# A two-layer decoder trunk on one core: the emptying of the values' bank written one step later, and the first quarter of the output products split by halves

## The chip, the cores and the metric

The kernel runs on one core of one Trainium2 chip. The metric is the device time of one execution in microseconds (us), the median over runs. TensorE (PE in the profile) does the matmuls, VectorE (DVE), ScalarE (ACT) and GpSimd (POOL) the elementwise work, and SyncE (SP) issues most transfers.

## The reference

The kernel computes two layers over 1024 tokens of width 1024, in float32. Each layer projects its input to a main part, memory queries and two gates, computes the main part and an attention over 256 memory tokens, multiplies both with their gates, projects back (the output products) and normalises. In the first layer the main part is a causal pooling. In the second it is an attention with 16 heads of 64 and a forget gate, and that is where the first half of the change lies:

```python
def block(args):                      # 128 queries at a time, all 16 heads
    logits = jnp.einsum('bqhd,bkhd->bhqk', qi, k) * scale
    logits = logits + (ci[..., :, None] - cum_k[:, :, None, :])
    logits = jnp.where(mask[None, None], logits, -jnp.inf)      # causal
    p = jax.nn.softmax(logits, axis=-1)
    return jnp.einsum('bhqk,bkhd->bqhd', p, v)
...
y = jnp.concatenate([y_main * silu(g_main), y_mem * silu(g_mem)], axis=-1)
x = layer_norm(ALPHA * x + y @ w_out, ln_g, ln_b)
```

## The kernel before

To keep float32's precision, each operand is split into a high part and a remainder, and each product is a sum of two or three cheaper matmuls. In the output products the parts are called `hi` (fp32r), `lo` (the remainder, bfloat16) and `top` (a bfloat16 copy); the three terms are hi x hi ("high"), and top x lo and lo x top ("low_top").

**The attention** is the function `fox`. It runs over 16 heads, and in each head over 8 steps, one for each tile of 128 queries, from tile 7 down to tile 0. Tile i has (i + 1) x 128 keys, cut into one or two parts of at most 512 columns (`parts_at`). A step does the following:

- `mask` (L1009, GpSimd) prepares the masked forget rows of a tile three steps ahead.
- `probs` computes the logits on TensorE (L323, two matmuls for each part, into one of three banks "L"), then on VectorE the scaled and masked logits with their running minimum (L1035), which frees the bank, and then on ScalarE the exponentials (L1043) into one of two banks "T". Between the two it normalises the tile of the step before (`inverse`, and `halves`: a scaled copy on ScalarE, L1071, and its remainder on VectorE, L1072).
- `fill.pump` places matmuls of projections (L359) between, so that TensorE always has work; their weights are split on GpSimd (L176, L193, L178).
- `turn` issues the transposing transfer of the probabilities (SyncE, L1088).
- Six steps after its tile, `values` multiplies the transposed probabilities with the values (L1097). It does so for four tiles at a time, so in two steps of each head, and accumulates in the bank "O", of which there is one. Behind the matmuls it empties the bank with what is called the join here: ScalarE scales one half of the partitions into `o` (L1114), and VectorE adds the other half (L1115).
- After the second head of a pair, `pair_out` multiplies `o` with its gate on GpSimd (L1124) and, after the second four tiles, stores it to `y1d` (SyncE, L1126).

After the last head six more steps finish the values, and the output products of the memory part's first quarter (`lead`) serve as filling.

**The output products** (`OutProj.rest`) run over four quarters `sp` of two 128-row tiles each and over three chunks `c` of the mixed channels. For each pair (sp, c) they load 4 x 128 x 256 values to `src`, split them with `hi_lo` (ScalarE L198 for `hi`, VectorE L199 for `lo`, ScalarE L200 for `top`), and issue 48 matmuls (L599). The quarter's first chunk 2 is done early, by `lead`, so `rest` begins with (0, 0). For chunk 0 the low and top terms come first, for the others the high terms.

**What sets the order.** TensorE's order in the second layer is the written one (`manual_schedule(engines={PE})`). The queues of the other engines are put together at compile time by a planner, which issues, of the instructions that it takes to be ready, the one that was written first. `tc.keep_in_program_order` (also called `pin`) holds an instruction behind the one written before it on the same engine. The join is not pinned; the masks and the gating are.

Of the kernel before, what the change touches and what calls it, by code (L numbers as in the profile page):

```python
# [9 lines left out]
F32 = mybir.dt.float32  # L10
# [4 lines left out]
AF = mybir.ActivationFunctionType  # L15
ALU = mybir.AluOpType
AX = mybir.AxisListType

P = 128
# [3 lines left out]
ST = S // P  # L23
NH = 512
HEADS = 16
# [47 lines left out]
def run(units):  # L73
    for _ in units:
        pass
# [3 lines left out]
def trunk_kernel(ctx, tc, x, xT, memT, win, wk, wv0, wv, wmk, wmv, wout, poolw, pscale, lng, lnb, bforget, out):  # L79
# [5 lines left out]
    nc = tc.nc  # L85
# [109 lines left out]
    def hi_lo(to, src, pinned=False, top=None):  # L195

        pin = tc.keep_in_program_order if pinned else lambda ins: ins
        pin(nc.scalar.copy(to.hi, src))  # L198
        pin(nc.vector.tensor_tensor(to.lo, src, to.hi.bitcast(F32), ALU.subtract))  # L199
        pin((top or nc.scalar.copy)(to.top, src))  # L200
# [343 lines left out]
    class OutProj:  # L544
# [36 lines left out]
            accs = [ps([P, NH], *bank) for bank in banks]  # L581
            return accs[:2], accs[2:]

        def products(self, accs, c, ys, apart=False):

            high, low_top = (0,), (1, 2)
            if apart:
                order = [(a, nh, part) for a in range(2) for part in (high, low_top) for nh in range(2)]
            else:
                order = [  # L590
                    (a, nh, part) for part in ((low_top, high) if c == 0 else (high, low_top))
                    for a in range(2) for nh in range(2)
                ]
            for a, nh, part in order:
                for i in part:
                    for k in range(4):
                        kt = 4 * c + k
                        y, w = three(ys[:, k, a * P : (a + 1) * P], self.ws[nh][kt // 2][kt % 2])[i]
                        nc.tensor.matmul(  # L599
                            accs[a][nh], y, w, start=kt == 8 and i == 0, stop=kt == 7 and i == 2,  # L600
                        )
                        yield NH
# [12 lines left out]
        def rest(self, resid, X, dst):  # L615
            order = [(sp, c) for sp in range(ST // 2) for c in (2, 0, 1)]
            accs, splits, gb = {}, [24], []
            if self.accs:
                accs[0], order[:6], splits = self.accs, [(0, 0), (1, 2), (0, 1), (1, 0), (1, 1)], [16, 24]
            if X is not None:  # L620
                self.split(splits.pop())

            def loads():

                for v in (lng, lnb):
                    t = sb([P, D], "P", 4)
                    nc.sync.dma_start(t, v[self.l].partition_broadcast(P))
                    gb.append(t)

            for sp, c in order:  # L630
                if c == 2:
                    accs[sp] = self.open((("T", 2), ("T", 2), ("L", 3), ("O", 1))) if 0 in accs and sp == 1 else self.open()
                src, ys = T([P, 4, 2 * P], F32), parts_of(T, [P, 4, 2 * P])
                nc.sync.dma_start(src, self.yd[c, :, :, sp * 2 * P : (sp + 1) * 2 * P])
                hi_lo(ys, src)
                if splits:
                    self.split(splits.pop(0), X is None)
                if not gb and not splits:
                    loads()
                if c == 1:  # L640
                    zs = rows_of(resid, sp)
                run(self.products(accs[sp], c, ys, X is None and sp == ST // 2 - 1 and c == 1))
                if X is not None and (sp, c) == (0, 0):
                    scale_of_norm(gb)
                if X is not None and c == 0 and sp:
                    scales_of_weights(sp - 1)
                if X is not None and c == 0 and sp in (1, 2):
                    keep(sp - 1)
                if c == 1:
                    norm(sp, accs.pop(sp), gb, zs, X, dst)  # L650
# [40 lines left out]
    X = parts_of(stream, [P, KT, S])  # L691
# [110 lines left out]
    X = X1  # L802
    with tc.tile_pool(name="in1", bufs=1) as in1:
# [165 lines left out]
        gs = {}  # L969
# [49 lines left out]
        def probs(hd, i, R, sums, inverse, behind):  # L1019

            q, kx, ky = pairs[hd // 2][hd % 2]
            qs = slice(i * P, (i + 1) * P)
            p = MK([P, S], F32)
            C, parts = diagonal.pop((hd, i)), parts_at(i)
            m = tiny(2)
            top = -NEG  # L1030
            for n, (lo, up) in enumerate(parts):
                lg = ps([P, NH], "L", 3)[:, : up - lo]
                mm3(lg, ((q[:, qs], kx[:, lo:up]), (q[:, qs], ky[:, lo:up])))
                rows = C[:, : up - lo] if n == len(parts) - 1 else R[:, lo:up]
                nc.vector.tensor_tensor_reduce(p[:, lo:up], lg, rows, unq, top, ALU.add, ALU.min, m[:, n : n + 1])  # L1035
                top = m[:, n : n + 1]
                if n == 0:
                    inverse()
            behind()
            es = []  # L1040
            for n, (lo, up) in enumerate(parts):
                e = ps([P, NH], "T", 2)[:, : up - lo]
                nc.scalar.activation(  # L1043
                    e, p[:, lo:up], AF.Exp, bias=top, scale=-1.0, accum_out=sums[:, n, hd % 2, i : i + 1],
                )
                es.append((lo, up, e))
            return hd, i, es, sums
# [42 lines left out]
        def values(hd, c, o):  # L1090

            v, un, b = pairs[hd // 2][2], unv if hd >= 4 else unv0, hd % 2
            acc = ps([P, NH], "O", 1)
            blocks = [(i, j) for i in range(4 * c, 4 * c + 4) for j in range(i + 1)]

            def add(rows, i, j, e, first, last):
                nc.tensor.matmul(  # L1097
                    acc[rows, (i % 4) * P : (i % 4) * P + P], v[:, b, 2 * j : 2 * j + (1 if e else 2), :].rearrange("p e d -> p (e d)"),
                    pt[hd, i][:, e * (i + 1) + j, :], start=first, stop=last,
                )  # L1100

            def highs(opens):
                for i, j in blocks:
                    add(slice(0, P), i, j, 0, opens and (i, j) == blocks[0], not opens and (i, j) == blocks[-1])

            def lows(opens):
                for k, (i, j) in enumerate(blocks):
                    add(slice(64 * (k % 2), 64 * (k % 2) + 64), i, j, 1, opens and k < 2, not opens and k >= len(blocks) - 2)

            for n, part in enumerate((lows, highs) if c else (highs, lows)):  # L1110
                part(n == 0)
            own, other = slice(64 * b, 64 * b + 64), slice(64 - 64 * b, P - 64 * b)
            oc = o[own, c * NH : (c + 1) * NH]
            nc.scalar.activation(oc, acc[other, :], AF.Copy, scale=un[own])  # L1114
            nc.vector.scalar_tensor_tensor(oc, acc[own, :], un[own], oc, ALU.mult, ALU.add)  # L1115

        bfb = const.tile([P, HEADS], F32, name="bfb")
        nc.sync.dma_start(bfb, bforget.partition_broadcast(P))
# [1 line left out]
        def pair_out(pr, c, o, g):  # L1120

            for k in (2 * c + 1, 2 * c) if g is not None else ():
                cols = slice(k * 2 * P, (k + 1) * 2 * P)
                tc.keep_in_program_order(nc.gpsimd.tensor_tensor(o[:, cols], o[:, cols], g[:, cols], ALU.mult))  # L1124
            if c == 0:
                nc.sync.dma_start(y1d[pr // 4, :, pr % 4, :], o)  # L1126
# [13 lines left out]
        def fox(following, out_proj, head):  # L1140
            fill, past, fresh = Fill(), [None] * LAG, [None]

            def two_lines(row):
                return [lines[0][:, row + j, :].bitcast(F32) for j in range(2)]

            ahead_R = forget_rows(0)
            for i in range(3):
                mask(0, ST - 1 - i, ahead_R)
            for hd in range(HEADS + 1):
# [16 lines left out]
                for i in range(ST if hd < HEADS else LAG):  # L1166
# [12 lines left out]
                    def behind():  # L1179
                        if fresh[0]:  # L1180
                            split.append(halves(*fresh[0]))
                            fresh[0] = None
# [21 lines left out]
                    if hd < HEADS:  # L1204
                        new = (hd, tile_of, o)
                        fresh[0] = probs(hd, tile_of, R, sums, inverse, behind)
                    else:
                        inverse()
                        behind()
                        out_proj.split(11 + i, True, gp_copy)  # L1210
                        if i > 1:
                            out_proj.fetch_two(two_lines(4 + 2 * i))
# [6 lines left out]
                        turn(*what)  # L1219
                    older = past[0]  # L1220
                    if older and older[1] % 4 == 0:
                        values(older[0], older[1] // 4, older[2])
                        if older[0] % 2:
                            pair_out(older[0] // 2, older[1] // 4, older[2], gs.get(older[0] // 2))
                    fill.pump(part * (1 - FRAC[0]))
                    past = past[1:] + [new]
                if b or hd == HEADS:
# [76 lines left out]
```

## Time and profile before

| | |
|---|---|
| time of three runs | 1190.94 us median (1190.53 to 1192.67) |
| profiled execution, its own time | 1189.29 us |
| its span | 1187.6 us |
| TensorE / VectorE / ScalarE / GpSimd busy | 98% / 66% / 58% / 24% of the span |
| granted TensorE clock, mean | 0.995 |
| attention | from about 640 us to 1060 us |
| output products of the second layer | from 1061 us |

Rows of the profile give a start and a duration in us, the engine, the line of the kernel, the operation, and the tiles it writes and reads (output<-inputs) with the shape. A bracket at the end is the idle time of the engine ahead of the instruction and what ended it. "PEld" is TensorE's loading of weights, which overlaps its matmuls. A group such as "x4" shows the time from the first start to the last end.

### The profile page before, as it was taken

To read this page: it belongs to the slowest core of one execution; us is meant where nothing else is said; L and a number is where in the kernel's file an instruction comes from. 1 tells how busy PE (TensorE), PEld (TensorE's weight loads), DVE (VectorE), ACT (ScalarE), POOL (GpSimd) and SP (SyncE) were. 2 spreads that over 40 slices of the span, in tenths; PEclk is the share of its full clock that TensorE was granted. 3 is DMA by queue.
4 is the path that set the end of the run, shared out by engine and by line. 5 is a ranking of instruction groups with operands and counts; after the bars stand their busy time and mean duration, and the time that the engine had idled before them with its cause. 6 is when DMAs were issued, how large, how long until landed. Compare 5 with 4: busy or idle time off the path is not lost. (4 is left out here: it accounts for less than half of the span.)

```text
span 1187.6 us, 19845 instructions
## 1 busy us (share of the span) xinstructions
PE 1165.6 (98%) x6941; PEld 671.7 (57%) x6941; DVE 779.1 (66%) x1840; ACT 684.8 (58%) x1512; POOL 285.5 (24%) x437
## 2 busy tenths in 40 slices
PE   8999999999999999999999999999999999999996
PEld 5566776555555557556674555555555545455553
DVE  5744675555765567457655888778877787874654
ACT  6578875976563234467422776667766667764210
POOL 3321001310000000000012454555555444750000
PEclk9999999999999999999999999999999999999998
DMA  7576646754385554446734889989996899875530
GB/s 257 182 242 193 170 105 213 245 180 144 91 279 162 158 148 131 122 134 117 192 130 113 181 187 208 202 167 198 204 207 145 168 196 203 215 193 168 176 108 35
DMA packets 286196, 203.89 MB, mean 172 GB/s; under 512 B 224912, under 2 KB 238352, under 8 KB 286096
## 3 DMA queue, kind: packets, MB, share of 16 engines
q1 hardware_dynamic: 279696, 181.59, 60.9%
q0 software_dynamic: 6400, 21.04, 5.5%
q8 instruction: 54, 0.88, 0.3%
q14 instruction: 46, 0.38, 0.1%
HBM read 116.01 MB, written 22.61 MB: 117 GB/s over the span
## 5 line engine op out<-in xcount | busy, mean ns | idle before, releaser
L359 PE MATMUL pj<-A,w 128*128 128x512 f16 (+2 forms) x2896 | 663.0, 382 | 3.3 <-ACT w L198 0.8
L359 PEld LDWEIGHTS <-w 128*128 128x128 f16 (+1 forms) x2560 | 245.4, 98 | 279.9 <-issue 9.6
L1043 ACT ACTIVATE T<-MK,s 128x512 f32<-128x512 f32 x192 | 111.2, 579 | 64.6 <-DVE s L1035 47.6
L1072 DVE SCALAR_TENSOR_TENSOR P<-T,s,P 128x512 f16<-128x512 f32 x192 | 111.9, 612 | 39.1 <-ACT P L1071 38.0
L1071 ACT ACTIVATE P<-T,s 128x512 f16<-128x512 f32 x192 | 103.0, 575 | 53.3 <-issue 28.9
L599 PEld LDWEIGHTS <-T 128*128 128x128 bf16 x736 | 70.7, 98 | 88.8 <-issue 4.4
L1009 POOL TENSOR_SCALAR_AFFINE_SELECT raw<-R 128x256 f32<-128x256 f32 (+3 forms) x128 | 59.3, 465 | 178.6 <-DVE s L1035 97.7
L323 PE MATMUL L<-A 128*128 128x512 f16 (+3 forms) x384 | 84.4, 326 | 3.1 <-DVE s L1035 3.0
L199 DVE TENSOR_TENSOR w<-raw,w 128x512 bf16<-128x512 f32 x74 | 51.9, 702 | 54.2 <-ACT w L198 39.3
L892 POOL MEMSET G<- 128x128 f32 x1 | 0.2, 204 | 333.7 <-DVE V L541 333.7
L359 PEld LDWEIGHTS pj<-A,w 128*128 128x128 f32 x352 | 65.1, 188 | 17.4 <-ACT w L198 1.9
L199 DVE TENSOR_TENSOR T<-T,T 128x1024 bf16<-128x1024 f32 x23 | 28.1, 1220 | 71.0 <-PE pj L599 37.3
L178 POOL TENSOR_TENSOR w<-B,w 128x512 f16<-128x512 f32 x54 | 62.8, 1165 | 4.0
L323 PEld LDWEIGHTS <-A 128*128 128x128 f16 x384 | 37.3, 98 | 46.2 <-issue 4.8
L198 ACT CAST T<-T 128x1024 fp32r<-128x1024 f32 x23 | 24.1, 1047 | 64.0 <-DMA T<-y1d 35.4
L198 ACT CAST w<-raw 128x512 fp32r<-128x512 f32 x76 | 46.7, 615 | 24.4 <-DMA raw<-in_win_dram 10.8
L1097 PEld LDWEIGHTS <-V 128*64 128x64 f16 (+1 forms) x1152 | 50.6, 104 | 13.0 <-issue 5.6
L1097 PE MATMUL O<-T,V 128*64 128x128 f16 (+1 forms) x1152 | 57.5, 220 | 0.0
L599 PE MATMUL pj<-B,T 128*128 128x512 bf16 (+1 forms) x192 | 53.0, 385 | 0.0
L1035 DVE CUSTOM_DVE_ANT_0 MK<-L,R,scales 128x512 f32<-128x512 f32 x64 | 45.3, 708 | 9.8 <-PE L L323 9.4
L200 ACT CAST w<-raw 128x512 bf16<-128x512 f32 x78 | 48.2, 618 | 3.3 <-PE pj L359 1.9
L599 PE MATMUL L<-B,T 128*128 128x512 bf16 (+1 forms) x168 | 47.4, 394 | 1.1 <-ACT T L200 1.1
(289 smaller groups left out, 1844.3 us busy)
## 6 DMA issues: line engine op xcount, KB each, us to landing
raw<-in_win_dram SPq DMA_DIRECT2D x66, 256.0 KB, 3.4
W<-in_win_dram POOLq DMA_DIRECT2D x48, 256.0 KB, 4.1
R<-cumd SPq DMA_DIRECT2D x16, 512.0 KB, 4.5
B<-in_win_dram SPq DMA_DIRECT2D x15, 512.0 KB, 5.2
y0d<-Y SPq DMA_DIRECT2D x12, 512.0 KB, 4.3
raw<-in_wout_dram SPq DMA_DIRECT2D x24, 256.0 KB, 2.6
T<-y0d SPq DMA_DIRECT2D x12, 512.0 KB, 4.7
A<-A SPq DMA_DIRECT2D x24, 256.0 KB, 4.0
```

The source lines that it names most:

```text
L178: pin(nc.gpsimd.tensor_tensor(to.lo, src, to.hi, ALU.subtract))
L198: pin(nc.scalar.copy(to.hi, src))
L199: pin(nc.vector.tensor_tensor(to.lo, src, to.hi.bitcast(F32), ALU.subtract))
L200: pin((top or nc.scalar.copy)(to.top, src))
L323: nc.tensor.matmul(acc, a, b, start=i == 0, stop=i == len(terms) - 1)
L359: nc.tensor.matmul(accs[n], a[:, k, :], b[:, pc * 4 + k, n * NH : (n + 1) * NH], start=seen[n] == 1, stop=seen[n] == 3 * KT,)
L599: nc.tensor.matmul(accs[a][nh], y, w, start=kt == 8 and i == 0, stop=kt == 7 and i == 2,)
L1009: tc.keep_in_program_order(nc.gpsimd.affine_select(C[:, :w], R[:, lo:up], [[-1, w]], ALU.is_ge, -NEG, base=w - P, channel_multiplier=1,))
L1043: nc.scalar.activation(e, p[:, lo:up], AF.Exp, bias=top, scale=-1.0, accum_out=sums[:, n, hd % 2, i : i + 1],)
L1071: nc.scalar.activation(pair[:, lo:up], e, AF.Copy, scale=r)
L1072: nc.vector.scalar_tensor_tensor(pair[:, L + lo : L + up], e, r, pair[:, lo:up], ALU.mult, ALU.subtract)
L1097: nc.tensor.matmul(acc[rows, (i % 4) * P : (i % 4) * P + P], v[:, b, 2 * j : 2 * j + (1 if e else 2), :].rearrange("p e d -> p (e d)"), pt ...
```

## The change

The change has two parts. In the attention `values` no longer writes the join; it returns it as a function, and `fox` keeps it with its step in a list `unjoined`. The new function `joins` writes the join and, for the second head of a pair, `pair_out`. It is called behind the next step's `probs`. In the six steps after the last head it is called as soon as the values' matmuls are written.

In `rest` the pair (0, 0) of the second layer, whose chunk 2 was done early, splits its input by halves of 128 rows: two `hi` casts, each followed by its remainder, and then two `top` casts, all pinned. Its products take the high terms first.

```diff
-        def products(self, accs, c, ys, apart=False):
+        def products(self, accs, c, ys, apart=False, high_first=True):
...
-                    (a, nh, part) for part in ((low_top, high) if c == 0 else (high, low_top))
+                    (a, nh, part) for part in ((low_top, high) if not high_first else (high, low_top))
...
-                hi_lo(ys, src)
+                joins = bool(self.accs) and (sp, c) == (0, 0)
+                if joins:
+                    pin = tc.keep_in_program_order
+                    tiles = [(ys[:, :, a * P : (a + 1) * P], src[:, :, a * P : (a + 1) * P]) for a in range(2)]
+                    for to, y in tiles:
+                        pin(nc.scalar.copy(to.hi, y))
+                        pin(nc.vector.tensor_tensor(to.lo, y, to.hi.bitcast(F32), ALU.subtract))
+                    for to, y in tiles:
+                        pin(nc.scalar.copy(to.top, y))
+                else:
+                    hi_lo(ys, src)
...
-                run(self.products(accs[sp], c, ys, X is None and sp == ST // 2 - 1 and c == 1))
+                run(self.products(accs[sp], c, ys, X is None and sp == ST // 2 - 1 and c == 1, joins or c > 0))
...
-            nc.scalar.activation(oc, acc[other, :], AF.Copy, scale=un[own])
-            nc.vector.scalar_tensor_tensor(oc, acc[own, :], un[own], oc, ALU.mult, ALU.add)
+
+            def join():
+                nc.scalar.activation(oc, acc[other, :], AF.Copy, scale=un[own])
+                nc.vector.scalar_tensor_tensor(oc, acc[own, :], un[own], oc, ALU.mult, ALU.add)
+
+            return join
...
+            unjoined = []
+
+            def joins():
+                while unjoined:
+                    join, (h, k, o) = unjoined.pop()
+                    join()
+                    if h % 2:
+                        pair_out(h // 2, k // 4, o, gs.get(h // 2))
...
                         fresh[0] = probs(hd, tile_of, R, sums, inverse, behind)
+                        joins()
                     else:
                         inverse()
                         behind()
+                        joins()
...
-                        values(older[0], older[1] // 4, older[2])
-                        if older[0] % 2:
-                            pair_out(older[0] // 2, older[1] // 4, older[2], gs.get(older[0] // 2))
+                        unjoined.append((values(older[0], older[1] // 4, older[2]), older))
+                        if hd == HEADS:
+                            joins()
```

## Prediction

> **What bounds the kernel now.** I read the first part of the page, then TensorE's waits after the start of the forgetting attention (640 us) and after 1061 us, then the timeline around each wait. The page first:
>
> ```profile
> span 1187.6 us, 19845 instructions
> PE 1165.6 (98%) x6941; PEld 671.7 (57%) x6941; DVE 779.1 (66%) x1840; ACT 684.8 (58%) x1512; POOL 285.5 (24%) x437
> ```
>
> TensorE is busy for 98% of the span, so only 22 us of it are idle, and an edit that takes no matmul away can save only idle time of TensorE. Two rows of the view of waits (wait, total us, times, longest us) are where this change can reach:
>
> ```profile
> PE L L323 <- DVE s L1035: 3.0, 6, 1.1
> PE L L599 <- ACT T L200: 1.1, 1, 1.1
> ```
>
> The first row is from the attention. The logits' matmuls (L323) wait for one of the three banks "L", which the running minimum on VectorE (L1035) gives back. The second is the start of the output products. The timeline shows the first wait in one head (start, us, engine, line; idle time in brackets):
>
> ```profile
> 718.40 0.81 PE L323 MATMUL L<-A 128*128 128x512 f16 x4
> 719.44 1.41 DVE L1072 SCALAR_TENSOR_TENSOR P<-T,s,P 128x512 f16<-128x512 f32 x2 [0.80 <-ACT P L1071]
> 720.01 0.69 ACT L1114 ACTIVATE G<-O,scales 64x512 f32<-64x512 f32 x1
> 720.77 0.73 DVE L1115 SCALAR_TENSOR_TENSOR G<-O,scales,G 64x512 f32<-64x512 f32 x1
> 721.20 0.49 PE L323 MATMUL L<-A 128*128 128x384 f16 x2
> 721.42 0.73 DVE L1035 CUSTOM_DVE_ANT_0 MK<-L,R,scales 128x512 f32<-128x512 f32 x1
> 722.22 0.38 PE L323 MATMUL L<-A 128*128 128x256 f16 x2 [0.53 <-DVE s L1035]
> ```
>
> The four matmuls at 718.40 are the logits of tile 5. They have ended at 719.21. Their first minimum starts only at 721.42, because two remainders (L1072) and then the join's second half (L1115) stand before it in VectorE's queue. TensorE needs that bank for the second part of tile 4 and stands still until 722.22. So L1115 holds a bank that TensorE needs, and nobody needs its own result here. The same steps in another head:
>
> ```profile
> 742.84 1.41 DVE L1072 SCALAR_TENSOR_TENSOR P<-T,s,P 128x512 f16<-128x512 f32 x2 [0.80 <-ACT P L1071]
> 744.16 0.74 DVE L1035 CUSTOM_DVE_ANT_0 MK<-L,R,scales 128x512 f32<-128x512 f32 x1
> 745.17 0.76 DVE L1115 SCALAR_TENSOR_TENSOR G<-O,scales,G 64x512 f32<-64x512 f32 x1 [0.26 <-ACT G L1114]
> 746.96 0.71 PE L323 MATMUL L<-A 128*128 128x384 f16 x4
> ```
>
> Here the minimum stands directly behind the remainders and ahead of L1115, and the four matmuls of tile 4 run through without a wait. This head has longer steps, so it is not a clean trial, but it shows that VectorE's queue takes the minimum at this point as soon as L1115 is not chosen first.
>
> **Part one: the join behind the next step's exponentials.** It adds and removes no work in the attention. It writes the two join instructions (and, for odd heads, the gating on GpSimd and for the second half the store on SyncE) after the next step's minima, remainders and exponentials. Of 32 joins 30 move; the last two still follow their matmuls at once. TensorE's order is written by hand and stays. On VectorE and ScalarE an instruction that is written later gives way only where a rival is ready, so I take it that at 720.77 L1035 goes first and L1115 after it.
>
> What is that worth? The listed idle time is not all that is lost: the undisturbed four matmuls of tile 4 take 0.71, the disturbed ones 721.20 to 722.60, which is 1.40. The loss is 0.69, 0.16 more than the listed 0.53. The minimum can move ahead by at most the start-to-start of L1115 and L1035, 721.42 - 720.77 = 0.65. The other waits of this kind, each with the join before it:
>
> ```profile
> 697.24 0.76 DVE L1115 SCALAR_TENSOR_TENSOR G<-O,scales,G 64x512 f32<-64x512 f32 x1
> 698.84 0.38 PE L323 MATMUL L<-A 128*128 128x256 f16 x2 [0.27 <-DVE s L1035]
> 823.36 0.73 DVE L1115 SCALAR_TENSOR_TENSOR G<-O,scales,G 64x512 f32<-64x512 f32 x1
> 824.82 0.38 PE L323 MATMUL L<-A 128*128 128x256 f16 x2 [0.43 <-DVE s L1035]
> 925.96 0.73 DVE L1115 SCALAR_TENSOR_TENSOR G<-O,scales,G 64x512 f32<-64x512 f32 x1
> 927.41 0.38 PE L323 MATMUL L<-A 128*128 128x256 f16 x2 [0.44 <-DVE s L1035]
> 967.56 0.48 PE L323 MATMUL L<-A 128*128 128x384 f16 x2 [0.25 <-DVE s L1035]
> 973.46 0.73 DVE L1115 SCALAR_TENSOR_TENSOR G<-O,scales,G 64x512 f32<-64x512 f32 x1
> 974.91 0.38 PE L323 MATMUL L<-A 128*128 128x256 f16 x2 [1.12 <-DVE s L1035]
> ```
>
> The wait at 967.56 has no join before it; I leave it. The five others lose their idle time plus 0.16: 0.43, 0.69, 0.59, 0.60 and 1.28, together 3.59. Capped at 0.65 each, the change recovers 0.43 + 0.65 + 0.59 + 0.60 + 0.65 = 2.92 us. Of the last, 0.63 stays. What is late next is VectorE's second minimum of tile 5, and TensorE needs its bank only in the step behind, some 2.5 us later (718.40 to 721.20 is a step of 2.8), so the 0.73 us of L1115 fit there. Once regained, time stays regained, because TensorE waits for little else. I cost nothing for the bank "O", which is emptied later: the next values' matmuls in it are these:
>
> ```profile
> 728.59 1.12 PE L1097 MATMUL O<-T,V 128*128 128x128 f16 x20
> ```
>
> L1115 ended at 721.50, so 7.09 us are spare against a delay of about one step. If that cover were gone, each microsecond beyond it would be paid by TensorE. The Trainium skill speaks against this edit here ("PSUM — Partial Sum Buffer", section "Summary: rules for kernel authors": evacuate promptly, because PSUM is tight); I weigh it as the last rival.
>
> The cost that I cannot read off is on GpSimd, which has the masks, the weights' splits and the gating in one queue:
>
> ```profile
> 759.51 1.41 POOL L1124 TENSOR_TENSOR G<-G,G 128x256 f32<-128x256 f32 x2 [2.24 <-DVE G L1115]
> 763.09 2.27 POOL L178 TENSOR_TENSOR w<-B,w 128x512 f16<-128x512 f32 x2
> 764.33 3.19 PE L359 MATMUL pj<-A,w 128*128 128x512 f16 x14
> ```
>
> GpSimd waits 2.24 us for L1115 and then finishes a weight piece (half of the 2.27, so at about 764.23) only 0.1 before TensorE starts on it. The move puts the next step's mask ahead of the gating, which uses the idle time and helps. A later L1115 hurts if the splits stay behind the gating. The bounds are a gain of 0 (TensorE does not wait here now) and a loss of one step, 2.8. I take 0, because the 2.24 of idle time in front of the gating holds much of such a delay, and keep 2.8 for the range. SyncE's stores move with the gating; the transposes that share its queue are issued several steps ahead of the values that need them, so I cost them at nothing.
>
> **Part two: the first quarter of the output products.**
>
> ```profile
> 1058.48 0.39 PE L1097 MATMUL O<-T,V 128*64 128x128 f16 x8
> 1058.91 1.04 ACT L198 CAST T<-T 128x1024 fp32r<-128x1024 f32 x1 [5.34 <-DMA T<-y1d]
> 1059.25 0.59 PE L599 MATMUL pj<-B,B 128*128 128x512 bf16 x2
> 1059.86 1.04 ACT L200 CAST T<-T 128x1024 bf16<-128x1024 f32 x1
> 1059.98 1.23 DVE L199 TENSOR_TENSOR T<-T,T 128x1024 bf16<-128x1024 f32 x1 [3.68 <-ACT T L198]
> 1060.95 0.61 PE L599 MATMUL L<-B,T 128*128 128x512 bf16 x2 [1.11 <-ACT T L200]
> 1063.30 0.68 ACT L1114 ACTIVATE G<-O,scales 64x512 f32<-64x512 f32 x1
> 1064.01 0.62 ACT L198 CAST R<-A 128x512 fp32r<-128x512 f32 x1
> 1064.53 0.61 ACT L200 CAST R<-A 128x512 bf16<-128x512 f32 x1
> ```
>
> The pair at 1059.25 takes 0.59 with two matmuls of about 0.38, so their starts lie 0.21 apart and the next could start at 1059.67. It starts at 1060.95: 1.28 lost, since the low and top terms come first and need two whole casts (1058.91 to 1060.90). After the change the high terms come first and need half a cast. A cast of 512 takes 0.62, its next starts 0.52 later. But the casts are pinned behind what is written before them on ScalarE, and that is the last join, which now stands at 1063.30. It can run when the values end, 1058.87. So: L1114 1058.90 to 1059.58, the first half's cast 1059.50 to 1060.12, TensorE from about 1060.15. That recovers 0.80. The second half's cast (about 1060.64) is there before the first half's eight high matmuls end; low and top parts follow by 1062 and are needed after sixteen. Bounds: 1.28 if the join does not stand in front; 0 if the join waits for something else on the way. I take 0.80, the rows' own times. Cost: two casts become four, 4 x 0.52 against 2 x 0.95, or 0.2 us of ScalarE, hidden beneath 48 matmuls. The last join's result comes some 4 us earlier, which only helps the quarter that reads it:
>
> ```profile
> 1077.28 1.04 ACT L198 CAST T<-T 128x1024 fp32r<-128x1024 f32 x1 [4.85 <-DMA T<-y1d]
> 1082.03 0.81 PE L599 MATMUL L<-R,T 128*128 128x512 f32 x2
> ```
>
> Its cast is ready 3.7 us before TensorE asks, and after 1061 us the view of waits names no other wait of TensorE. So the 0.80 reaches the end.
>
> **Sum.** 2.92 + 0.80 = 3.72 us. The profiled execution took 1189.29 us (span 1187.6), so it would come to 1185.6. The three timed runs have a median of 1190.94, 1.65 above it; I carry the difference over: 1190.94 - 3.72 = 1187.2.
>
> **Rivals.**
> First, the join keeps its place. The queue is made at compile time; if the minimum is not held to be ready when L1115 is, the order stays as it is and only part two counts: 1190.94 - 0.80 = 1190.1. For it: the last join stands behind casts that were written later (1063.30), so the planner's idea of when things are ready differs from the chip's. Against it: at 744.16 it takes the minimum at this very point, and on the chip the logits have been there for 1.5 us.
>
> Second, GpSimd takes the wait over: the gating holds up the weights at 764.33 by a step, 2.8. That gives 1187.2 + 2.8 = 1190.0. For it: a spare of 0.1. Against it: one place only, and 2.24 of idle time before it.
>
> Third, slower: ScalarE's half of the join takes the wait's place.
>
> ```profile
> DVE P L1072 <- ACT P L1071: 38.0, 62, 0.8
> ```
>
> VectorE waits 62 times for ScalarE's scaled copies (L1071), and what stands behind it in the queue, minima included, waits too. If L1114 (0.69) lands in front of such a copy in the step behind, its minima move by about 0.65 there. That can be at each of the 15 first joins that move: 15 x 0.65 = 9.8, giving 1197.0. To outweigh 3.7 and the 2.4 of a measurable change it needs ten of them. For it: 38.0 us of such waits. Against it: most heads have no wait of TensorE at all, so they have slack for it.
>
> Fourth, the bank: the join sinks so far behind ready work that the next values' matmuls find "O" full. It decides from 7.1 us of delay, over two steps; at 8 us, were all 30 places as the one shown, 30 x 0.9 = 27, or 1214. That is what the page's rule would make of it. Against it: VectorE is busy for 66% of the span, so there is room within a step.
>
> **How the numbers follow.** About 0.2%, or 2.4 us, can be told from no change. Chances: forecast 0.58 (faster), order kept 0.17 and GpSimd 0.08 (both within 0.2%), ScalarE's half 0.13 and the bank 0.04 (slower). Faster 0.58, same 0.25, slower 0.17. The forecast's own range: 3.59 + 1.28 = 4.87 at best gives 1186.1, and 2.4 at least gives 1188.5. The range must take in the second and third cases (1190.1) and something for the spread of the runs (1190.53 to 1192.67): 1185.0 to 1191.5, which leaves the slower cases out.
>
> **What would show it.** Right: L1035 directly behind the second L1072 where L1115 now stands, the wait for L1035 down from 3.0 to about 0.8 (0.25 and some 0.5 of the longest one), and the first output product starting with high terms 0.8 earlier, behind L1114. Wrong: the same order with the same waits; TensorE waiting for L178 or L193 near 764; longer waits of L1072 for L1071 with new waits of TensorE behind them; or L1097 waiting for L1115.

## The result, and the profile after

The kernel with the change takes 1192.12 us (median of 22 runs, 1190.13 to 1193.9); the kernel before took 1190.76 in as many runs on the same chips. The ratio is 1.0014 [1.0007, 1.0020]: slower by 0.14%, where 1187.2 us and a gain were forecast. The profiled execution took 1192.17 us.

The page's first rows:

```profile
span 1190.5 us, 19846 instructions
PE 1166.6 (98%) x6941; PEld 672.2 (56%) x6941; DVE 779.0 (65%) x1841; ACT 684.9 (58%) x1514; POOL 284.5 (24%) x437
```

TensorE's waits after 640 us (wait, total us, times, longest us):

```profile
PE L L323 <- DVE s L1045: 6.2, 7, 1.5
PE pj L359 <- POOL w L193: 0.5, 1, 0.5
PE L L599 <- ACT T L640: 0.4, 1, 0.4
```

Line numbers have moved: the running minimum is L1045 (was L1035), the remainders L1082 (L1072), the join's halves L1126 and L1127 (L1114, L1115), the values' matmuls L1107 (L1097). Hardly any engine's busy time has changed (TensorE's by 1.0 us). The wait for the running minimum, which the change was expected to bring from 3.0 to about 0.8 us, is 6.2.

Two runs cannot be compared by their whole spans here: the time up to the attention's first logits matmul differs from run to run by more than the effect (644.3 to 647.6 us over all kernels below, by waits of TensorE near 8, 480 and 602 us that no edit touches). So I cut each trace at the start of the first logits matmul of every pair of heads. "Last" is the time from the last logits matmul to the first output product of `rest`; "whole" is from the start of the attention's first logits matmul to the start of the kernel's last matmul. Each trace is one execution, so the columns say what happened in that one, and the time says what the runs did together.

| us | pair 0 | pair 1 | pair 3 | pair 5 | pair 6 | pair 7 | last | whole |
|---|---|---|---|---|---|---|---|---|
| before | 42.58 | 47.05 | 46.41 | 46.42 | 47.50 | 54.39 | 18.50 | 531.93 |
| after | 42.35 | 47.02 | 46.43 | 46.43 | 48.05 | 56.42 | 17.83 | 533.73 |

Pairs 2 and 4 take 56.18 us in both. So part one won 0.26 us (pairs 0 and 1), part two 0.67, and 0.55 and 2.03 were lost in pairs 6 and 7, in which nothing had been expected to get longer; 0.11 more lies behind the first output product.

**Where the order stayed.** VectorE and TensorE in the head that the prediction took as its example, after:

```profile
719.95 1.41 DVE L1082 SCALAR_TENSOR_TENSOR P<-T,s,P 128x512 f16<-128x512 f32 x2 [0.81 <-ACT P L1081]
721.28 0.73 DVE L1127 SCALAR_TENSOR_TENSOR G<-O,scales,G 64x512 f32<-64x512 f32 x1
721.93 0.73 DVE L1045 CUSTOM_DVE_ANT_0 MK<-L,R,scales 128x512 f32<-128x512 f32 x1
722.73 0.38 PE L323 MATMUL L<-A 128*128 128x256 f16 x2 [1.04 <-DVE s L1045]
```

L1127 still stands ahead of L1045, although it is now written behind it. The same holds near 824, 926 and 974. Only near 676 and 698 did the two change places:

```profile
696.34 1.41 DVE L1082 SCALAR_TENSOR_TENSOR P<-T,s,P 128x512 f16<-128x512 f32 x2 [0.81 <-ACT P L1081]
697.67 0.74 DVE L1045 CUSTOM_DVE_ANT_0 MK<-L,R,scales 128x512 f32<-128x512 f32 x1
698.45 0.76 DVE L1127 SCALAR_TENSOR_TENSOR G<-O,scales,G 64x512 f32<-64x512 f32 x1
698.50 0.71 PE L323 MATMUL L<-A 128*128 128x384 f16 x4
```

There TensorE's four matmuls run through in 0.71 us, as forecast. But look at the next such place, 722.73: its listed wait grew from 0.53 to 1.04. TensorE came earlier by what it had won, VectorE did not, and most of the 0.43 won at 698 was given back one head later.

**Where new time is lost.** TensorE in head 13 (pair 6) and in head 15 (pair 7), after:

```profile
968.65 0.48 PE L323 MATMUL L<-A 128*128 128x384 f16 x2 [0.80 <-DVE s L1045]
1021.76 0.59 PE L323 MATMUL L<-A 128*128 128x512 f16 x2
1023.23 0.48 PE L323 MATMUL L<-A 128*128 128x384 f16 x2 [0.87 <-DVE s L1045]
1032.26 0.38 PE L323 MATMUL L<-A 128*128 128x256 f16 x2 [1.50 <-DVE s L1045]
```

The wait in head 13 is the one that the prediction left alone, listed with 0.25 before and 0.80 after: it is the whole 0.55 of pair 6. VectorE reaches it later. Its first minimum of head 12 starts 2.32 us behind the start of its logits (2.08 before), since one more remainder (L1082, 0.35 us) stands ahead of it. A few steps on it waits 1.10 us for a scaled copy (0.80 before), and from there it is 0.54 later than before.

The two waits in head 15 were not there before. With the 0.16 that a listed wait leaves out they cost 1.03 and 1.66. VectorE and GpSimd just ahead of them, with TensorE's matmuls beside them, first before, then after:

```profile
1016.75 1.66 POOL L193 TENSOR_SCALAR w<-B 128x512 f16<-128x512 f32 x2
1017.25 1.71 DVE L199 TENSOR_TENSOR MK<-A,MK 128x512 bf16<-128x512 f32 x2
1018.39 2.70 POOL L178 TENSOR_TENSOR w<-B,w 128x512 f16<-128x512 f32 x2
1020.03 1.47 PE L359 MATMUL pj<-A,w 128*128 128x512 f16 x6 [0.70 <-POOL w L178]
1020.40 0.80 DVE L1035 CUSTOM_DVE_ANT_0 MK<-L,raw,s 128x512 f32<-128x512 f32 x1
1021.33 0.92 PE L323 MATMUL L<-A 128*128 128x512 f16 x4
```

```profile
1015.45 0.76 DVE L1127 SCALAR_TENSOR_TENSOR G<-O,scales,G 64x512 f32<-64x512 f32 x1
1018.06 1.20 POOL L193 TENSOR_SCALAR w<-B 128x512 f16<-128x512 f32 x2
1019.23 2.72 POOL L178 TENSOR_TENSOR w<-B,w 128x512 f16<-128x512 f32 x2
1019.36 3.14 DVE L199 TENSOR_TENSOR MK<-A,MK 128x512 bf16<-128x512 f32 x2
1023.69 0.80 DVE L1045 CUSTOM_DVE_ANT_0 MK<-L,raw,s 128x512 f32<-128x512 f32 x1
```

L199 here is the remainder of two pieces of the output products' weights, an instruction that the change does not touch. Its two instructions (the L199 pair from here on) take 1.71 us before and 3.14 after. Before, the pair starts in front of GpSimd's last L193, and GpSimd is the one that takes longer (1.66 where after has 1.20). After, GpSimd's L178 starts 0.13 us ahead of it, and VectorE is the one. As a result the second minimum, which stood 0.93 us ahead of TensorE's logits (1020.40 against 1021.33), now stands 1.93 behind them (1023.69 against 1021.76). Half of that shift of 2.86, 1.43, is the longer L199. VectorE also starts L199 1.03 later against the first logits of head 15 (2.11 us behind them, 1.09 before), and the moved join of head 13 (L1127 at 1015.45; L1115 at 1012.40 before) now stands shortly ahead of it. Behind L199, 0.25 of this is caught up. And TensorE comes 0.65 earlier: its wait for L178 (0.70 listed at 1020.03, 0.86 in all) is gone, and a wait for L193 near 1018 is 0.22 longer. In TensorE's time this is 1.03 + 1.66 - 0.86 + 0.22 = 2.05, the loss of pair 7.

**The start of the output products**, after:

```profile
1060.87 1.12 PE L1107 MATMUL O<-T,V 128*128 128x128 f16 x20
1062.04 0.68 ACT L1126 ACTIVATE G<-O,scales 64x512 f32<-64x512 f32 x1 [5.35 <-PE O L1107]
1062.74 1.14 ACT L640 CAST T<-T 128x512 fp32r<-128x512 f32 x2
1063.41 0.73 PE L599 MATMUL L<-B,T 128*128 128x512 f32 x2 [0.45 <-ACT T L640]
```

The steps are those of the forecast: the join first, half a cast, then high terms. TensorE starts 1.42 us after the values' end (1061.99 to 1063.41), where 1.28 was worked out.

### The profile page after: what moved, and what is told of

It is laid out like the page before. It is cut to its first block, busy times and chain, and to the rows that moved or that the text cites. A ratio compares the mean times of both kernels' runs of the same rounds, so it can differ in the third digit from the quotient of the medians.

```text
span 1190.5 us, 19846 instructions
## 1 busy us (share of the span) xinstructions
PE 1166.6 (98%) x6941; PEld 672.2 (56%) x6941; DVE 779.0 (65%) x1841; ACT 684.9 (58%) x1514; POOL 284.5 (24%) x437
## 5 line engine op out<-in xcount | busy, mean ns | idle before, releaser
L1082 DVE SCALAR_TENSOR_TENSOR P<-T,s,P 128x512 f16<-128x512 f32 x192 | 111.6, 613 | 39.3 <-ACT P L1081 38.2
L1081 ACT ACTIVATE P<-T,s 128x512 f16<-128x512 f32 x192 | 102.7, 576 | 56.4 <-issue 34.7
L199 DVE TENSOR_TENSOR w<-raw,w 128x512 bf16<-128x512 f32 x74 | 51.9, 701 | 54.4 <-ACT w L198 39.2
L199 DVE TENSOR_TENSOR T<-T,T 128x1024 bf16<-128x1024 f32 x22 | 26.8, 1220 | 65.6 <-PE pj L599 43.8
L178 POOL TENSOR_TENSOR w<-B,w 128x512 f16<-128x512 f32 x54 | 62.9, 1166 | 3.7
L1107 PEld LDWEIGHTS <-V 128*64 128x64 f16 (+1 forms) x1152 | 50.6, 104 | 12.9 <-issue 5.7
L1107 PE MATMUL O<-T,V 128*64 128x128 f16 (+1 forms) x1152 | 57.5, 220 | 0.0
L1045 DVE CUSTOM_DVE_ANT_0 MK<-L,R,scales 128x512 f32<-128x512 f32 x64 | 45.3, 708 | 8.9 <-PE L L323 8.5
```

Source lines behind the costliest of these rows:

```text
L178: pin(nc.gpsimd.tensor_tensor(to.lo, src, to.hi, ALU.subtract))
L1081: nc.scalar.activation(pair[:, lo:up], e, AF.Copy, scale=r)
L1082: nc.vector.scalar_tensor_tensor(pair[:, L + lo : L + up], e, r, pair[:, lo:up], ALU.mult, ALU.subtract)
L1107: nc.tensor.matmul(acc[rows, (i % 4) * P : (i % 4) * P + P], v[:, b, 2 * j : 2 * j + (1 if e else 2), :].rearrange("p e d -> p (e d)"), pt ...
```

## The experiments

In the order in which they ran. "Whole" and "last" are the columns of the table above.

**Each part alone.** `b_only` writes every join at once, as before, and keeps part two; `a_only` keeps the joins of the change and takes part two away:

```diff
-                        if hd == HEADS:
-                            joins()
+                        joins()                     # b_only
...
-                joins = bool(self.accs) and (sp, c) == (0, 0)
+                joins = False                       # a_only
```

> Part two alone: every join is written at once behind its matmuls, as before; the first quarter of the output products is split by halves. Theory (the attention loses what part two gains): the attention's waits are those of the kernel before (3.0 us in 6 waits for L's minimum), the first output product waits about 0.5 instead of 1.1, and the time is 0.6 us below before (ratio 0.9995). Rival (part two itself disturbs the queues of the attention): waits for the minimum near 6 us as in the changed kernel, time 1 to 2 us above before.

> Part one alone: joins moved as in the change, the output products as before. Theory: about 2 us above before (the changed kernel's 1.4 and the 0.6 of part two), waits for the minimum near 6 us with the long ones behind 1020 us. Rival (the loss is part two's): the time of before within 0.5 us.

`b_only`: 1.0005 [0.9995, 1.0015] of before; whole 531.49, last 17.83, all pairs as before. `a_only`: 1.0015 [1.0006, 1.0024]; whole 533.23, pair 6 48.03, pair 7 56.49. So all of the loss is part one's. That part two alone is a gain rests on the trace (whole 0.44 us less than before); the time does not show the 0.6 us that were expected.

One number did not fit. In `a_only` the last stage is 17.39: 1.11 shorter than before without part two, and 0.44 shorter than after with it. The loads of the quarter show why. Before:

```profile
1053.43 1.51 SPq L634 DMA_DIRECT2D T<-y1d  x2
1057.75 1.12 PE L1097 MATMUL O<-T,V 128*128 128x128 f16 x20
```

with the cast at 1058.91, whose row stands in the prediction; and `a_only`:

```profile
1056.43 1.82 SPq L634 DMA_DIRECT2D T<-y1d  x2
1062.01 1.12 PE L1107 MATMUL O<-T,V 128*128 128x128 f16 x20
1062.05 1.04 ACT L198 CAST T<-T 128x1024 fp32r<-128x1024 f32 x1 [4.23 <-DMA T<-y1d]
```

The loads are issued 4.32 us ahead of the values' group of 20 before, and 5.58 ahead of it with part one, so the cast, which waits for the data, can start 1.12 us earlier. So with part one most of the wait that part two was made for is gone. SyncE's queue comes to these loads earlier: the transpose ahead of them takes 2.11 us before (at 1050.60) and 1.21 in `a_only` (at 1053.28). Which of the moved instructions brings this about was not isolated. Part two then put the join, which must wait for the values, in front of a cast whose data were there. Alone it wins 0.67; on top of part one it costs 0.44 in the traces, too little for the times to show (1.0014 and 1.0015).

**Which joins bring the loss of pair 7.** `ab_to11` moves only the joins of heads 0 to 11, `ab_from12` only those of 12 to 14:

```diff
-                        if hd == HEADS:
+                        if hd == HEADS or older[0] >= 12:     # ab_to11; ab_from12: < 12
```

> The change, but the joins of heads 12 to 15 are written at once as before. Theory (the loss comes late: the moved joins of the last two pairs shift VectorE's work so that two weight remainders of the output products run beside GpSimd's splits, and TensorE then waits about 2.7 us near 1023 and 1032 us): the two late waits go, the time is about 0.5 to 1 us below before. Rival (the loss is spread over the heads, by delayed joins in general): time still 1 us above before.

> The change with the joins of heads 0 to 11 written at once and only those of heads 12 to 14 moved. Theory (timing of VectorE against GpSimd at the end of head 14 decides, and any small shift of VectorE brings the collision): the last pair takes 55 to 56.5 us against 54.4 before. Rival (only moved joins of the earlier heads matter): 54.4.

`ab_to11`: 0.9993 [0.9983, 1.0003]; whole 533.61, pair 7 56.21. `ab_from12`: 1191.26 us in one run; whole 533.50, pair 7 56.43. In the traces each half alone brings nearly the whole loss, so the late joins as such are not its cause, and the two halves do not add up. The theory for `ab_to11` missed: both late waits of TensorE stayed (1.12 and 1.54 listed). What the halves have in common is the long L199 pair (`ab_to11`, then `ab_from12`):

```profile
1018.53 2.71 POOL L178 TENSOR_TENSOR w<-B,w 128x512 f16<-128x512 f32 x2
1018.53 3.27 DVE L199 TENSOR_TENSOR MK<-A,MK 128x512 bf16<-128x512 f32 x2
```

```profile
1018.28 2.72 POOL L178 TENSOR_TENSOR w<-B,w 128x512 f16<-128x512 f32 x2
1018.41 3.14 DVE L199 TENSOR_TENSOR MK<-A,MK 128x512 bf16<-128x512 f32 x2
```

In `b_only`, without the loss, L199 starts 1.14 us ahead of L178 and the pair takes 1.71, as before.

`ab_to11` isolates this best, because no join of pair 7 is moved in it. Up to 1.3 us ahead of the first logits of head 15, VectorE's rows lie where they lie before, within 0.01 us. What differs is GpSimd's start on a piece that a transfer brings (before, then `ab_to11`):

```profile
1015.00 1.78 POOL L176 TENSOR_SCALAR B<-B,scales 128x512 f32<-128x512 f32 x2 [4.01 <-DMA B<-in_win_dram]
```

```profile
1015.60 1.79 POOL L176 TENSOR_SCALAR B<-B,scales 128x512 f32<-128x512 f32 x2 [3.71 <-DMA B<-in_win_dram]
```

The logits start at 1016.16 and 1017.06, so L176 is 1.16 us ahead of them before and 1.46 here. It now starts ahead of another L199, which takes 1.07 for 0.69, and the L199 pair follows with 3.27 for 1.71. Together these two make VectorE's first minimum of head 15 lag 4.93 us behind its logits, 2.98 before. `b_only` and `b_split` issue this transfer at the same time against the logits, and there L176 starts 1.02 and 1.01 ahead. So the moment at which a transfer lands varies by more than what decides the order, and another execution of `ab_to11` may fall the other way. Its times do not show the loss that its trace has (0.9993; the trace has 1.68 more than before).

Pair 6 separates the halves: 48.05 in `ab_to11`, 47.52 in `ab_from12`. Its 0.55 does come from the joins up to head 11.

**The order forced.** `ab_pinned` takes VectorE's half of the join behind the step's first minimum and holds it there. ScalarE's half stays where it was before, and the second joins of each head are written at once:

```diff
+            nc.scalar.activation(oc, acc[other, :], AF.Copy, scale=un[own])
-            def join():
-                nc.scalar.activation(oc, acc[other, :], AF.Copy, scale=un[own])
-                nc.vector.scalar_tensor_tensor(oc, acc[own, :], un[own], oc, ALU.mult, ALU.add)
+            def join(pin=lambda ins: ins):
+                pin(nc.vector.scalar_tensor_tensor(oc, acc[own, :], un[own], oc, ALU.mult, ALU.add))
...
+                    first()        # in probs, behind a tile's first minimum: joins(tc.keep_in_program_order)
...
-                        if hd == HEADS:
+                        if hd == HEADS or older[1] // 4 == 0:
```

> ScalarE's half of each join stays directly behind the matmuls; VectorE's half of a head's first join is held in program order directly behind the next step's first minimum; the second join of each head stays where it was; part two kept. This forces the order that the forecast had taken for granted. The forecast's step: the waits for the minimum at about 698, 722, 825, 927 and 975 us shrink by 0.4 to 0.65 each, 2.9 in all, and with part two the time is 3.5 us below before. Rival (VectorE paces these heads, so TensorE only comes further ahead of it and waits later): single waits shrink, but others grow, and no more than 1.5 us of the 2.9 stays.

0.9984 [0.9974, 0.9994]; whole 530.31, the pairs 42.35, 46.41, 45.82 (pair 3), 45.82 (pair 5), 47.35 and 55.49. Near 824, in this kernel and then in the one after:

```profile
824.28 0.74 DVE L1045 CUSTOM_DVE_ANT_0 MK<-L,R,scales 128x512 f32<-128x512 f32 x1
824.78 0.71 PE L323 MATMUL L<-A 128*128 128x384 f16 x4
824.94 0.73 DVE L1129 SCALAR_TENSOR_TENSOR G<-O,scales,G 64x512 f32<-64x512 f32 x1
```

```profile
823.88 0.73 DVE L1127 SCALAR_TENSOR_TENSOR G<-O,scales,G 64x512 f32<-64x512 f32 x1
824.54 0.73 DVE L1045 CUSTOM_DVE_ANT_0 MK<-L,R,scales 128x512 f32<-128x512 f32 x1
825.33 0.38 PE L323 MATMUL L<-A 128*128 128x256 f16 x2 [0.45 <-DVE s L1045]
```

With the minimum first, the wait is gone. Pairs 0 to 6 win 2.21 us together, between the 2.9 of the theory and the 1.5 of the rival, so the mechanism of the prediction works where the order is the one that it took for granted. Two waits are left that it had counted as won or had left alone: 0.43 listed at 723.12 (0.53 before), and the one near 967, which cost 0.41 before and costs 0.80 here. Pair 7 of the heads still loses 1.10, beside an L199 pair of 3.26 us.

**The weights' splits moved.** To take L199 away from L178, `ab_split` writes the splits of these two pieces five steps later, with the joins of the change:

```diff
-                        out_proj.split((0, 0, 0, 0, 1, 3, 4, 6, 6, 6, 6, 6, 7, 8, 9, 10)[step], True, gp_copy)
+                        out_proj.split((0, 0, 0, 0, 1, 3, 4, 4, 4, 4, 4, 4, 6, 8, 9, 10)[step], True, gp_copy)
```

Here, and in `pinned_split` and `pinned_split_last` below, two pieces of the output weights are overwritten by the next ones before they are split, so the output products use other weights there; the number of recorded matmuls is the same (6894). `ab_split2` and the kernels after it also load the next ones one step later (13 for 12) and compute all of it.

> The change, with the two weight splits that fell in the last step of head 14 (rows 5 and 6 of the output weights) written five steps later, in a light step of head 15. Theory (these two remainders on VectorE run beside GpSimd's subtractions and take 1.6 us each instead of 0.7 to 1.1, so VectorE enters head 15 two microseconds late, and TensorE pays it at the next full bank): the last pair of heads takes about 54.4 us instead of 56.4, VectorE's lag at the start of head 15 falls from 5.0 to below 3.5, the time is about 0.5 us below before. Rival (the lag at head 15 comes from the moved joins of heads 13 and 14 themselves): the last pair still takes 56 us and the time stays 1.4 us above before.

> As ab_split, with the transfer that refills the rows of those two weights moved from step 12 to step 13, so that the split reads them first. Theory: last pair 53.8 us as in ab_split, and the time 0.2 to 0.3 us below before. Rival (ab_split was quick because of the weights that it missed): the last pair is back at 56 us.

`ab_split`: 1.0005 [0.9994, 1.0017], whole 531.67, pair 7 53.81. `ab_split2`: 0.9991 [0.9981, 1.0000], whole 531.37, pair 7 53.79. Pair 7 falls from 56.42 by 2.6 in both, so the weights that `ab_split` did not use are not why. The time of `ab_split` was not below before, as its theory had it; that of `ab_split2` is, at the edge of its interval. GpSimd and VectorE in `ab_split2`, at the place where L199 was:

```profile
1019.76 2.28 POOL L178 TENSOR_TENSOR w<-B,w 128x512 f16<-128x512 f32 x2
1020.05 0.74 DVE L1045 CUSTOM_DVE_ANT_0 MK<-L,R,scales 128x512 f32<-128x512 f32 x1
1021.32 0.80 DVE L1045 CUSTOM_DVE_ANT_0 MK<-L,raw,s 128x512 f32<-128x512 f32 x1
```

L178 takes 2.28 with nothing in its way. Against the first logits of head 15 (1017.72 here, 1017.25 after) the second minimum comes 2.83 us earlier than after. Is that a repair of the change's cost, or a gain of its own? `b_split` makes the same move without part one:

> Part two and the later split alone, every join at once as before. Theory (the later split only takes away the collision, which the kernel before mostly lacks): last pair 54.4 or up to 0.6 less, time 0.5 to 1 us below before. Rival (the later split is a gain of its own of 2 us whatever the joins do): last pair 52.5, time 2.5 us below before.

0.9975 [0.9964, 0.9985]; whole 530.52, pair 7 53.51. The kernel before had some of this cost too, 0.88 us in pair 7 (54.39 to 53.51): its wait for L178 is gone. That speaks for the theory, while the time comes out nearer to the rival's 2.5 us; the trace has 1.41 of it. With part one, pair 7 is 53.79: of the 2.03 that it lost, 0.28 is left, and this is TensorE's wait for L193 near 1018 (0.52 listed in `ab_split2`, 0.24 in `b_split`). So 1.75 hung on L199 in that place. The move takes away the pair's own work there too, so how much of the 1.75 is the 1.43 of standing still is not separated by these runs; in `ab_to11`, where VectorE came as before, the longer L199s alone went with 1.82 in pair 7.

**All of it together.** `pinned_split` joins the forced order and the later splits:

> VectorE's half of each head's first join held behind the next step's first minimum, ScalarE's half and the second joins as before, the two weight splits five steps later, part two kept. Theory: the first twelve heads keep their gain of 2.1 us, the last pair goes from 55.5 to about 54.4; with part two the time is about 3 us below before (ratio 0.9975). Rival (VectorE's work only moves, and head 15 pays for the splits where it is fullest): the last pair stays at 55.5 and the time is 1.5 us below before.

0.9975 [0.9964, 0.9986]; whole 529.16, pair 7 54.39. That is 1.10 less than `ab_pinned` in pair 7, as much as `ab_pinned` had lost there, but still 0.88 above `b_split`. The two waits for the minimum in head 15 (1.12 and 0.50 listed in `ab_pinned`) are gone; in this trace TensorE waits 1.06 for L193 near 1017 instead, where `b_split` has 0.24. `pinned_split_last` was to take the last join from in front of the half casts:

```diff
                     for to, y in tiles:
                         pin(nc.scalar.copy(to.hi, y))
                         pin(nc.vector.tensor_tensor(to.lo, y, to.hi.bitcast(F32), ALU.subtract))
+                    last_join()
                     for to, y in tiles:
                         pin(nc.scalar.copy(to.top, y))
```

> As pinned_split, and the very last join is written behind the first quarter's high casts, ahead of the top casts. Theory: the first output product no longer waits 0.4 for the cast, 0.6 us less than pinned_split. Rival (the later join holds up the store that the third product group reads): another wait of TensorE takes its place near 1080 us and nothing is gained.

0.9981 [0.9969, 0.9993]; last stayed 17.84. The edit had moved VectorE's half only; ScalarE's, which stands in front of the cast, was still where it had been. So this run tells nothing of the wait. `pinned_split_last2` moves both halves of that one join:

> As pinned_split_last, with both halves of the very last join behind the high casts (the run before had moved only VectorE's half, and ScalarE's still stood in front), and the refill as in ab_split2. Theory: the wait of the first output product goes, 0.6 us less than pinned_split, and with the gains of heads 0 to 12 the time is 3.5 us below before (ratio 0.997). Rival (the later join holds up the store of the last pair): a wait of TensorE near 1080 us takes its place.

1185.67 us (median of 6, 1184.13 to 1186.93), 0.9953 [0.9939, 0.9966] of before: faster than both kernels. Whole 527.81, last 17.04, pair 7 53.79. The trace has 4.12 us less than before, of which 0.80 against `pinned_split` is the wait that this edit was made for, and 0.60 a shorter wait in pair 7 (0.52 near 1016). Its casts:

```profile
1055.09 1.14 ACT L640 CAST T<-T 128x512 fp32r<-128x512 f32 x2 [3.64 <-DMA T<-y1d]
1055.20 1.12 PE L1109 MATMUL O<-T,V 128*128 128x128 f16 x20
1056.94 0.81 PE L599 MATMUL L<-B,T 128*128 128x512 f32 x2
1057.69 0.68 ACT L1128 ACTIVATE G<-O,scales 64x512 f32<-64x512 f32 x1
```

and the first of TensorE's waits:

```profile
PE L L323 <- DVE s L1046: 1.5, 3, 0.6
```

The cast waits for its data alone and runs beside the values. TensorE, which has a few products of `lead` behind the values' group of 20, goes on to those of `rest` without a listed wait. The wait for the minimum is down to 1.5 from 3.0 before and 6.2 after.

## Why the prediction was wrong

**The step that failed** is "so I take it that at 720.77 L1035 goes first and L1115 after it". At four of the six places where a join stood in front of the minimum and TensorE lost time by it, it did not: at 721.28 L1127 still goes first. The first rival, that the join keeps its place, describes them. Why the planner keeps the order there and not at 676 and 698 stays open: the argument given for the rival, that its idea of readiness is not the chip's, fits, but no run tests it. The argument against the rival was a head with longer steps, in which the join itself still waited for ScalarE's half (0.26 listed at 745.17); that the prediction itself called it no clean trial should have lowered 0.58.

Between the forecast, 3.72 us less, and the trace after, 1.80 more, lie 5.5 us. The order that stayed is 2.7 of them (0.26 won for 2.92), the loss in pairs 6 and 7 is 2.6, and part two 0.1.

**The size of part one was nearly right.** With the order forced, the five places recovered 0.43 (698), 0.10 (722), 0.59, 0.60 and 0.65, where 0.43, 0.65, 0.59, 0.60 and 0.65 had been worked out; even the rest of the longest wait, 0.63, is there (974.47, 0.47 listed). A sixth place, 676, gave 0.24 that was not on the list. The step "once regained, time stays regained, because TensorE waits for little else" was too strong: at 722 and near 967 the matmuls wait for the same engine, and what is won upstream is partly paid there, 0.55 at 722 and 0.39 at 967. So the sum was 2.2 and not 2.92.

**What was missing was a cost** on an engine pair that the prediction treated as two queues. It bounded GpSimd's price by who stands behind whom (0 to 2.8), and never asked what runs beside VectorE. The moved join made L199 start 1.03 us later against TensorE, and that decided which of L199 and L178 started first. With L199 out of that place, 1.75 of the 2.03 of pair 7 are gone. `ab_to11` shows that the same loss can come without a late join there, from a transfer that lands 0.30 us earlier. The trace of before had the sign of it: L199's pair at 1.71 and L193's at 1.66 in one stretch, where L193's takes 1.20 a few us later. That the 0.55 of pair 6 comes from the joins up to head 11 is shown, and that it is paid at the wait near 967; which of the moved instructions makes VectorE late there was not isolated.

**Part two** was mis-sized by little: 0.67 for 0.80. From the join to the cast it takes 0.70 (1062.04 to 1062.74) where 0.60 had been allowed. That the two parts meet was overlooked: "SyncE's stores move with the gating ... so I cost them at nothing" left SyncE's queue out of the sum, and with it a gain of 1.1. With that gain in place part two's value is negative in the kernel after.

**The other rivals.** TensorE did not wait near 764. The third, ScalarE's half ahead of the scaled copies, did not come as it was described: that wait (L1082 for L1081) went from 38.0 us in 62 waits only to 38.2 in 59. A single such wait, 1.10 for 0.80, lies on the way to the loss of pair 6, but without L1126 in front of the copy. Nor did the fourth come: no L1107 waits for L1127. The page "PSUM — Partial Sum Buffer" of the Trainium skill, section "Summary: rules for kernel authors", would have the bank emptied promptly. Here VectorE's half of a join came up to 2.3 us later behind its matmuls than before (4.81 for 2.48 in head 1), at least 3.4 us were left to the next ones, and nothing waited. The slower outcome had a chance of 0.17, put on two mechanisms that are both wrong.

## What to carry to other kernels

To write an instruction later is to lower its priority, no more: read the order that results, and hold it in place if the gain depends on it. Time won against an engine that runs late is kept only if nothing behind waits for the same engine, so follow its lag to the next wait before adding up. Before moving anything on VectorE, list which two-input instructions on operands in SBUF run near GpSimd's, since the order of their starts decides which of them pays; 0.13 us ahead was enough here, less than the landing of a transfer varies.

## What the runs showed of the hardware

VectorE's two-input subtraction (L199) and GpSimd's instructions that read SBUF (L178, L193) do not slow each other by shares: the one that starts later stands still until the other is nearly done. In the kernel after, L178's two instructions and the second L199:

```profile
L178 POOL TENSOR_TENSOR w<-B,w x2: 1155/1378/1601, 1019.2 to 1020.4; 128x512 f16<-128x512 f32 x2
L199 DVE TENSOR_TENSOR MK<-A,MK x1: 1642/1642/1642, 1020.9 to 1020.9; 128x512 bf16<-128x512 f32 x1
```

The columns are the minimum, median and maximum of the duration in ns, and the first and last start. By single instructions in the trace: L178 runs undisturbed from 1019.23 to 1020.39 (1.155). L199 starts inside it, at 1019.36, and ends at 1020.94, 0.55 after it. The second L178 starts at 1020.35, inside L199, and ends 1.02 after that, at 1021.95 (1.601). The second L199 starts inside this one and ends 0.55 after it, at 1022.50 (1.642). Each one's duration is what is left of the other's, plus nearly its own; alone, L199 takes 0.68 to 0.69. The other gives way about 0.13 us ahead of its recorded end (0.68 less 0.55): an L199 that starts in the last 0.12 us of an L193 (1017.25 before) still takes 0.69. VectorE's minimum, which has one input in the bank "L", is not held up: it takes 0.73 beside the L178 that runs from 1018.39 to 1019.97 before. In the profile none of this is idle time: the blocked instruction looks like a long one.

The Trainium skill states this ("SBUF — State Buffer", section "Who interferes with whom"): a VectorE instruction with two inputs in SBUF and a GpSimd instruction that reads SBUF contend, and whoever issues first holds the ports for the whole instruction while the other is fully blocked. The trace agrees, in both directions: before, L199 came first at 1017.25 and GpSimd's L193 pair took 1.66; after, L193's pair took 1.20 undisturbed, and L199's 3.14.
